# Layer 0's values and layer 1's x into token form: 32x32 block transposes on VectorE and a pass through DRAM in place of transposes on TensorE

## The chip, the core and the metric

One core of a Trainium2 chip runs the kernel: TensorE (PE, its weight loads listed as PEld), VectorE (DVE), ScalarE (ACT), GpSimd (POOL) and SyncE (SP), which issues nearly all DMA. The metric is device time of one execution in microseconds. The kernel before was timed three times: 1389.19, 1389.40 and 1389.46 us, median 1389.4.

## The reference: what is computed

Two residual layers work on 272 tokens (16 learned meta tokens and 256 frames) of width 2048, in float32. Pad slots that the reference puts in front are masked there and are not stored by the kernel.

Layer 0 projects the tokens once and splits the result. Four heads of gated linear attention (GLA) have keys of 256 and values of 512; eight stick-breaking heads (SB) have width 128. In both, a matrix of scores between tokens multiplies the values `v`:

```python
o_intra = jnp.einsum('bchts,bcshv->bcthv', scores, v)
outs.append(jnp.einsum('bhqk,bhkd->bhqd', w, v[:, :, :k_len].astype(jnp.float32)))
```

Layer 1 is a Mamba-2 mixer (SSD) with 8 groups of 8 heads of 64. Its `x` is convolved over time, passed through SiLU, and multiplied by a step `dt` for each token and head; then a matrix of decays and scores multiplies it:

```python
xdt = x * dt[..., None]
y_diag = jnp.einsum('bctsgh,bcsghp->bctghp', l_mat * cb[..., None], xdt)
```

Each layer ends with an output projection, a residual and a layer norm.

In all three places the sum runs over source tokens `s`, so the values must lie with tokens on partitions ("token form"). The projections deliver them with channels on partitions. Something must transpose them.

## The kernel before

**Units and projections.** The weights come in units of 128x2048 floats (1 MB), in a list written out in the program. SP loads them ahead of use into three buffers `raw` (L144). ACT rounds each half of a unit to `whi` (L159); DVE, and for some late units POOL, takes the rest `wlo` (L160). There are five buffers of halves. A unit of an input projection gives 128 channels for all tokens: 16 slices of the contraction, three matmuls each (L178, L179, L180, the products hi·hi, hi·lo, lo·hi), 48 matmuls that add up in one PSUM bank `pj` with channels on partitions and 272 (or 256) tokens on columns. Output units of layer 1 are 24 matmuls of 512 columns (L494 to L496).

**What sets the order.** When a unit is done, its post function takes the PSUM bank over. What follows (attention, gates, the SSD scan) is written as generators, which are stepped once a quarter of a unit; a `yield` is thus a delay in the program's order. A scheduler then sets the final order of instructions on each engine, and each engine runs its own list strictly in order. An instruction that waits holds up whatever stands behind it on the same engine. This is also true of SP: a load that waits for a free buffer, or for another transfer to land, holds up the loads behind it.

**Values of layer 0.** `post_gv` (GLA, four units a head, worked off in pairs) and `post_sv` (SB, one unit a head) copy the bank to `vraw` on ACT (L623, L761). `to_tokens` transposes it on PE with the identity as the moving operand: two 128x128 blocks (L587) and the last 16 tokens (L588) for each unit, into a bank `po`. ACT rounds the result to `gvh` (L596, L592), DVE takes the rest `gvl` (L597 to L599). `values` (L608 and after) multiplies them with the score matrix.

**x of layer 1.** Four units of a group fill `xt`. The convolution and SiLU are done in pairs (DVE L1050, L1057, L1061). After the second pair `x_path` waits five more steps, transposes on PE (L1173, eight blocks; L1177, four of 16 tokens), and DVE multiplies each result straight out of PSUM by `dt` from `est` and `est2` into `xd` (L1186, four) and `xd2` (L1192, four). The SSD mix multiplies `M` by `xd` on PE (L1235). `M` is made on DVE and ACT (L1105, L1106, L1108) from `ebc`, a copy of the group's decays on all partitions, which SP loads from the DRAM tile `edr` (L1072) into the one buffer with the tag `hacc` (272 x 16 floats a partition; `ebc` fills 8 x 416 of these 4352).

In all there are 168 transposes on PE: 48 at L587, 24 at L588, 64 at L1173 and 32 at L1177.

## Time and profile before

| | |
|---|---|
| median of three runs | 1389.4 us |
| the profiled execution's own time | 1389.59 us |
| its span, first to last instruction | 1387.7 us |
| PE busy | 1379.2 us, 99% |
| DVE busy | 1017.3 us, 73% |
| ACT busy | 771.7 us, 56% |
| POOL busy | 260.6 us, 19% |
| granted TensorE clock | 1.000 |
| DMA over the span | 249.83 MB, mean 180 GB/s |

Layer 0 fills about the first half of the span; the first SSD transposes stand shortly after 763 us. Records of PE overlap: matmuls are pipelined, and a matmul's record is longer than the distance to the next one. What an instruction adds to PE's list is therefore read from the distance between starts. In a row of a timeline stand the start, the duration, engine, line, operation, output and inputs, shapes and count, and in brackets the idle time ahead of it and what ended it. In a row of groups stand the count, then the busy sum and the mean in ns, then idle time ahead. A DMA row gives the count, KB each and the median us from issue to landing.

### The profile page before, as it was taken

The numbers are of one execution on the slowest core, as the hardware profiler recorded it, in microseconds if no ns is written. First come the engines' busy times: TensorE is split into PE (matmuls) and PEld (weight loads), VectorE is DVE, ScalarE is ACT, GpSimd is POOL, SyncE is SP. The second block draws the span as 40 slices with busy tenths as digits, with TensorE's granted clock in tenths as the row PEclk, the third lists the DMA queues.
The fourth block names the chain that finished last, engine by engine and source line by source line (L and its number), as shares of the span: only waits on it lengthen the run. The fifth ranks groups of instructions, "written<-read, shape, count | busy, mean of one in ns | idle before, by whom it ended". The sixth has DMA issues, their size and how long they took to land.

```text
span 1387.7 us, 26097 instructions
## 1 busy us (share of the span) xinstructions
PE 1379.2 (99%) x10715; PEld 1328.3 (96%) x10715; DVE 1017.3 (73%) x1690; ACT 771.7 (56%) x1149; POOL 260.6 (19%) x253
## 2 busy tenths in 40 slices
PE   9999999999999999999999999999999999999998
PEld 8999999999999999999999999899898999989986
DVE  7857575574565565557899999787877778867687
ACT  6645454454345544556587677565565655656551
POOL 0000010100101000113500153331322323133221
PEclk9999999999999999999999999999999999999999
DMA  8544544445454445544354655465555556455561
GB/s 320 185 161 156 181 154 171 163 156 179 156 179 156 153 152 179 174 151 148 122 199 169 251 202 201 158 256 174 213 180 187 197 187 228 164 200 185 179 216 61
DMA packets 38007, 249.83 MB, mean 180 GB/s; under 512 B 4288, under 2 KB 6144, under 8 KB 9472
## 3 DMA queue, kind: packets, MB, share of 16 engines
q1 hardware_dynamic: 37168, 247.38, 51.0%
q8 instruction: 84, 1.38, 0.4%
q10 hardware_dynamic: 720, 0.79, 0.2%
q14 instruction: 35, 0.29, 0.1%
HBM read 245.94 MB, written 2.20 MB: 179 GB/s over the span
## 4 chain that ended last, share of the span: by engine, by line
PE 94%; DVE 3%; DMA 1%; ACT 1%; POOL 1%; issue 0%; SPq 0%; ACTq 0%; POOLq 0%; DVEq 0%
PE pj L179 25%; PE pj L178 25%; PE pj L180 25%; PE pj L494 4%; PE pj L496 4%; PE pj L495 4%; PE po L1235 1%; PE po L608 1%; DVE wlo L160 1%; PE po L1173 0%; DMA raw<-in_wts 0%; PE po L587 0%; PE z L1123 0%; POOL yu L1246 0%; DVE M L1105 0%
## 5 line engine op out<-in xcount | busy, mean ns | idle before, releaser
L178 PE MATMUL pj<-xhi,whi 128*128 128x272 f32 (+4 forms) x2560 | 732.1, 286 | 1.3 <-DVE fix L936 0.5
L179 PE MATMUL pj<-xlo,whi 128*128 128x272 f32 (+4 forms) x2560 | 730.8, 286 | 0.0
L180 PE MATMUL pj<-xhi,wlo 128*128 128x272 f32 (+4 forms) x2560 | 730.1, 286 | 0.0
L159 ACT ACTIVATE whi<-raw 128x1024 fp32r<-128x1024 f32 (+2 forms) x434 | 449.6, 1039 | 423.8 <-PE pj L179 350.7
L160 DVE TENSOR_TENSOR wlo<-raw,whi 128x1024 fp32r<-128x1024 f32 (+2 forms) x405 | 503.3, 1247 | 242.0 <-ACT whi L159 237.4
L178 PEld LDWEIGHTS pj<-xhi,whi 128*128 128x128 f32 x2560 | 482.1, 189 | 3.7 <-ACT whi L159 0.9
L179 PEld LDWEIGHTS pj<-xlo,whi 128*128 128x128 f32 x2560 | 482.1, 188 | 1.5 <-DVE wlo L160 0.4
L180 PEld LDWEIGHTS pj<-xhi,wlo 128*128 128x128 f32 x2560 | 481.9, 188 | 1.0 <-issue 0.8
L178 PE MATMUL pj<-mixh,whi 128*128 128x272 f32 x384 | 110.5, 289 | 0.0
L180 PE MATMUL pj<-mixh,wlo 128*128 128x272 f32 x384 | 110.5, 288 | 0.0
L179 PE MATMUL pj<-mixl,whi 128*128 128x272 f32 x384 | 110.4, 288 | 0.0
L160 POOL TENSOR_TENSOR wlo<-raw,whi 128x1024 fp32r<-128x1024 f32 x29 | 73.0, 2517 | 192.6 <-ACT whi L159 192.6
L494 PE MATMUL pj<-whi,yh 128*128 128x512 f32 (+1 forms) x240 | 93.3, 389 | 0.0
L495 PE MATMUL pj<-wlo,yh 128*128 128x512 f32 (+1 forms) x240 | 92.6, 386 | 0.0
L496 PE MATMUL pj<-whi,yl 128*128 128x512 f32 (+1 forms) x240 | 92.2, 386 | 0.0
L261 POOL TENSOR_TENSOR gr<-gr,gsc 128x1088 f32<-128x1088 f32 x6 | 15.4, 2568 | 308.2 <-ACT gsc L260 308.2
L179 PEld LDWEIGHTS pj<-mixl,whi 128*128 128x128 f32 x384 | 72.3, 188 | 0.2
L180 PEld LDWEIGHTS pj<-mixh,wlo 128*128 128x128 f32 x384 | 72.3, 188 | 0.1
L178 PEld LDWEIGHTS pj<-mixh,whi 128*128 128x128 f32 x384 | 72.2, 188 | 0.1
L503 DVE SCALAR_TENSOR_TENSOR acc<-pj,rr,acc 128x512 f32<-128x512 f32 (+1 forms) x65 | 46.5, 734 | 13.9 <-PE pj L496 13.9
L496 PEld LDWEIGHTS pj<-whi,yl 128*128 128x128 f32 x240 | 45.1, 188 | 9.1
L494 PEld LDWEIGHTS pj<-whi,yh 128*128 128x128 f32 x240 | 45.1, 188 | 9.0
(351 smaller groups left out, 1472.2 us busy)
## 6 DMA issues: line engine op xcount, KB each, us to landing
raw<-in_wts SPq DMA_DIRECT2D x212, 1024.0 KB, 4.8
ebc<-edr SPq DMA_DIRECT2D x8, 1664.0 KB, 6.7
raw<-in_wts SPq DMA_DIRECT2D x9, 256.0 KB, 6.4
hacc<-in_xT SPq DMA_DIRECT2D x7, 272.0 KB, 5.3
early<-in_wts SPq DMA_DIRECT2D x2, 512.0 KB, 6.5
lg<-in_lnr SPq DMA_DIRECT2D x1, 1024.0 KB, 4.7
lb<-in_lnr SPq DMA_DIRECT2D x1, 1024.0 KB, 5.3
out_h<-acc SPq DMA_DIRECT2D x2, 384.0 KB, 2.4
```

Of the source, the lines that this page charges most:

```text
L159: self.nc.scalar.activation(hi, src, AF.Copy)
L160: eng.tensor_tensor(lo, src, hi.bitcast(F32), op=ALU.subtract)
L178: mm(ps, whi, xhi, start=first, stop=False)
L179: mm(ps, whi, xlo, start=False, stop=False)
L180: mm(ps, wlo, xhi, start=False, stop=last)
L261: mul(c, c, e, op=ALU.mult)
L494: mm(ps, yh[:, kk, tt], hi[:, k, :], start=kk == 0, stop=False)
L495: mm(ps, yh[:, kk, tt], lo[:, k, :], start=False, stop=False)
L496: mm(ps, yl[:, kk, tt], hi[:, k, :], start=False, stop=kk == 3)
L503: self.nc.vector.scalar_tensor_tensor(a, ps, r[:, t : t + 1], a, op0=ALU.mult, op1=ALU.add)
L608: mm = lambda r, a, b, start=False, stop=False: self.nc.tensor.matmul(o[:, r], a, b, start=start, stop=stop, skip_group_check=True)
L1235: pin(mm(ov[p][i * 64 : (i + 1) * 64, jj, t0:S], xd[:, s, h * 64 : (h + 1) * 64], M[:, h, c0:c1], start=(s, jj) == (0, 0), stop=False, **gk,))
```

## The change

A transpose of 128x128 is made of two steps: transposing each 32x32 block in place on DVE, and then moving blocks between partitions, which DMA does by a pass through DRAM.

**Layer 0.** `v_blocks` transposes the blocks straight out of the projection's PSUM bank into `vt` (L586, 256 elements a partition; L587, the 32 columns that hold the last 16 tokens). There is one buffer `vt`, and no `vraw`. `to_tokens` then has SP write `vt` to a DRAM tile (L600, L601) and read it back in five parts: four for the 32-partition strips of the two big token tiles (L604; runs of 128 bytes for an SB head, 256 for a GLA pair), one for the last 16 tokens (L606). The reads come back into `vt` itself. ACT and DVE then split as before, from SBUF (L612 to L617).

**Layer 1.** `x_path` transposes after each of the two pairs (L1186, 512 elements a partition; L1187, 64). The result `xs` lies in the unused tail of the group's `ebc` buffer. After the second pair SP writes 512 KB and 64 KB (L1194, L1195), reads four parts back into `xs` (L1198, runs of 512 bytes) and two into `xd2` (L1202). DVE multiplies by `dt` from SBUF (L1214, four; L1221, two, in place). The five steps of delay are gone, and the wait for the step sizes is now a wait until the group's `ebc` has been asked for. `load_decay` of the next group, which takes the same buffer, comes behind the reads of this group. `est2` is held twice, at partitions 0 and 32, and `cpk` shrinks from 384 to 360 columns.

```diff
+    def v_blocks(self, ps, i, n):
+        if i == 0:
+            self.vt = self.lp.tile([P, 768], F32, tag="vt", name=self.nm("vt"))
+        o = self.vt[:, : 256 * n].rearrange("q (b c x) -> q b c x", c=n, x=32)[:, :, i, :]
+        self.nc.vector.transpose(o, ps[:, :256].rearrange("p (b x) -> p b x", x=32))
+        self.nc.vector.transpose(self.vt[:, 512 + 32 * i : 544 + 32 * i], ps[:, 240:T])
+        return self.vt
...
     def to_tokens(...):
-            for t in range(2):
-                nc.tensor.transpose(pts[i][:, t * P : (t + 1) * P], raw[:, t * P : (t + 1) * P], self.ident)
-            nc.tensor.transpose(pts[0][:16, 256 + i * P : 256 + (i + 1) * P], raw[:, 256:272], self.ident)
-        nc.scalar.activation(v2[:16, w], t2, AF.Copy)
-            nc.scalar.activation(vh[:, :, c], p, AF.Copy)
-            nc.vector.tensor_tensor(vl[:, :, c], p, vh[:, :, c].bitcast(F32), op=ALU.subtract)
...
+        sync.dma_start(d.rearrange("p t b x -> (p t) (b x)"), blk)
+        sync.dma_start(d9.rearrange("p t x -> (p t) x"), s9)
+        v = blk.rearrange("q (s p x) -> q s p x", s=2, p=4)
+        for b in range(4):
+            sync.dma_start(v[32 * b : 32 * b + 32], d[:, :, b::4].rearrange("p t s x -> t s p x"))
+        t2 = vt[:16, 512 : 512 + P * n].rearrange("q (p x) -> q p x", p=4)
+        sync.dma_start(t2, d9[:, 16:].rearrange("p t x -> t p x"))
+        yield
+        yield
...
+        act(chan(v2[:16, w]), cols(t2), AF.Copy)
+        for t in range(2):
+            act(chan(vh[:, t, w]), cols(v[:, t]), AF.Copy)
+            vec.tensor_tensor(chan(vl[:, t, w]), cols(v[:, t]), chan(vh[:, t, w].bitcast(F32)), op=ALU.subtract)
...
     def load_decay(self, g):
-        eb = self.hp.tile([P, HPG, 416], F32, tag="hacc", name=self.nm("ebc"))
+        eb = self.hp.tile([P, KT * T], F32, tag="hacc", name=self.nm("ebc"))
+        self.cur["xs", g] = eb[:, HPG * 416 :].rearrange("p (b c x) -> p b c x", c=4, x=32)
...
     def x_path(self, g, j):
-        if g == 0:
-            yield from _wait(self.tasks["dt"])
+        while ("ebc", g) not in self.cur:
+            yield
+        vec.transpose(xs[:, :, j : j + 2, :].rearrange("p b c x -> p c b x"), xt[:, j : j + 2, :S].rearrange("p c (b x) -> p c b x", x=32))
+        vec.transpose(x9[:, j : j + 2, :], xt[:, j : j + 2, 240:T])
+        yield
         if j == 0:
             return
-        for _ in range(5):
-            yield
...
+        nc.sync.dma_start(d.rearrange("p t b x -> (p t) (b x)"), xs.rearrange("q b c x -> q (b c x)"))
+        nc.sync.dma_start(d9.rearrange("p t c x -> (p t) (c x)"), x9.rearrange("q c x -> q (c x)"))
+        for b in range(4):
+            nc.sync.dma_start(
+                xb[32 * b : 32 * b + 32], d[:, :, b::4].rearrange("p t s x -> t s p x")
+            )
+        for i in range(2):
+            nc.sync.dma_start(
+                self.xd2[32 * i : 32 * i + 16].rearrange("t (n a) (b x) -> t n (a b) x", n=2, b=2),
+                d9[:, 16:, i::2].rearrange("p t n x -> t n p x"),
+            )
...
+                vec.tensor_tensor(o, x, e.broadcast_to([P, 4, 2, 32]), op=ALU.mult)
...
+            vec.tensor_tensor(x, x, e.broadcast_to([16, 2, 2, 64]), op=ALU.mult)
```

**Where instructions stand now.** SP gains seven DMA for each GLA pair and each SB head, and eight for each SSD group; its list goes from 256 rows to 352, rows of one kind side by side counted once. On SP at SB head 1 (`raw` are weight loads, `vt` the block-transposed values, `vdr` the DRAM tile) the changed program has:

```order
L144 DMA raw_5407<-in_wts 128x2048
L144 DMA raw_5504<-in_wts 128x2048
L144 DMA raw_5580<-in_wts 128x2048
L600 DMA vdr_5450<-vt_5404 128x256
L601 DMA vdr_659_5451<-vt_5404 128x32
L604 DMA vt_5404<-vdr_5450 32x8x32 x4
L606 DMA vt_5404<-vdr_659_5451 16x4x32
L144 DMA raw_5665<-in_wts 128x2048
```

Before, only the weight loads stood there. The writes now stand behind one weight load and the reads ahead of the next.

ACT at the same head, before:

```order
L761 ACTIVATE vraw_5378<-pj_5298 128x272
L572 ACTIVATE s0h_5372<-sbe_5336 128x432
L159 ACTIVATE whi_5513<-raw_5380 128x1024
L592 ACTIVATE v_148<-po_5423 16x128
L596 ACTIVATE gvh_5294<-po_5423 128x2x128
L803 ACTIVATE spad<-z_64 128x432
L159 ACTIVATE whi_5549<-raw_5470 128x1024
L745 ACTIVATE qe_5467<-pj_5382 128x272
```

and changed:

```order
L572 ACTIVATE s0h_5398<-sbe_5362 128x432
L159 ACTIVATE whi_5543<-raw_5407 128x1024
L818 ACTIVATE spad<-z_64 128x432
L159 ACTIVATE whi_5583<-raw_5504 128x1024
L761 ACTIVATE qe_5501<-pj_5409 128x272
L614 ACTIVATE gvh_5320<-vt_5404 128x128 x2
L612 ACTIVATE v_148<-vt_5404 16x128
L572 ACTIVATE s0h_5475<-spad 128x432
```

The copy to `vraw` is gone, and the split to `gvh` has moved behind the next unit's weight half and the next head's `qe`. On PE, 90 to 92 projection matmuls now stand between the end of an SB head's `sv` unit and its first matmul of values for heads 1, 2, 3, 5, 6 and 7 (80 to 104 before), and 104 for heads 0 and 4 as before.

DVE at SSD group 3, before:

```order
L1061 TENSOR_TENSOR xt_11029<-xt_11029,xcl_11279 128x544
L160 TENSOR_TENSOR wlo_11441<-raw_11327,whi_11440 128x1024
L160 TENSOR_TENSOR wlo_11479<-raw_11387,whi_11478 128x1024
L1057 TENSOR_SCALAR xcl_11420<-gz_11325 128x512
L1186 TENSOR_TENSOR xd_11030<-po_11406,est 128x256 x2
L1186 TENSOR_TENSOR xd_11030<-po_11407,est 128x256 x2
L1192 TENSOR_TENSOR xd_8126<-z_64,est_8718 16x128 x4
L160 TENSOR_TENSOR wlo_11507<-raw_11387,whi_11506 128x1024
```

and changed (`ebc_10958` here is its tail `xs`):

```order
L1077 TENSOR_TENSOR xt_11107<-xt_11107,xcl_11360 128x544
L1186 STREAM_TRANSPOSE ebc_10958<-xt_11107 128x2x8x32
L1187 STREAM_TRANSPOSE x_1359_11265<-xt_11107 128x64
L160 TENSOR_TENSOR wlo_11556<-raw_11484,whi_11555 128x1024
L1073 TENSOR_SCALAR xcl_11505<-gz_11408 128x512
L160 TENSOR_TENSOR wlo_11584<-raw_11484,whi_11583 128x1024
L160 TENSOR_TENSOR wlo_11617<-raw_11552,whi_11616 128x1024
L1214 TENSOR_TENSOR xd_11108<-ebc_10958,est 128x4x64 x4
L1221 TENSOR_TENSOR xd_8208<-xd_8208,est_8798 16x256 x2
```

The block transposes stand right behind the last SiLU product, and the products with `dt` have moved two weight halves further back. The writes and reads stand between the two on SP, the reads behind one more weight load:

```order
L1194 DMA xdr_11429<-ebc_10958 128x1024
L1195 DMA xdr_1379_11430<-x_1359_11265 128x128
L144 DMA raw_11659<-in_wts 128x2048
L1198 DMA ebc_10958<-xdr_11429 32x8x128 x4
L1202 DMA xd_8208<-xdr_1379_11430 16x8x32 x2
L144 DMA raw_11741<-in_wts 128x2048
L1090 DMA ebc_11901<-edr 128x3328
```

Before, the next group's decay load (L1072) stood behind this group's last read of `ebc` by DVE; now also behind the reads of x.

88 lines of the change are left out of this document (39 added, 49 removed).

## The prediction, on record before the changed kernel ran

> **What bounds the kernel now.** I read the page's busy row first, then the row of slices, then what PE waited for, then the busy time by stretches.
>
> ```profile
> PE 1379.2 (99%) x10715; PEld 1328.3 (96%) x10715; DVE 1017.3 (73%) x1690; ACT 771.7 (56%) x1149; POOL 260.6 (19%) x253
> DVE  7857575574565565557899999787877778867687
> PE po L1393 <- ACT diag L1328: 1.2, 1, 1.2
> ```
>
> PE is busy for 1379.2 of the span's 1387.7 us, and its longest wait is 1.2 us. So the kernel lasts as long as PE's list of instructions, and an instruction taken off PE is worth its own length, as long as nothing else is the limit where it stood. The slices say where that is in doubt: DVE stands at 9 in slices 22 to 25, some 730 to 870 us. Cut into windows (window, length, then busy time and instructions of PE, weight loads, DVE, ACT and POOL, then clock, DMA share, GB/s):
>
> ```profile
> 730.00:760.00 30.00, 29.17 (x245) 28.42 (x243) 28.78 (x55) 21.51 (x35) 3.01 (x3) 1.00 0.49 170
> 760.00:790.00 30.00, 30.00 (x237) 27.69 (x238) 29.20 (x59) 21.60 (x30) 4.72 (x3) 1.00 0.63 232
> 790.00:830.00 40.00, 39.80 (x358) 37.84 (x355) 39.67 (x81) 27.21 (x46) 18.53 (x12) 1.00 0.59 207
> 890.00:975.00 85.00, 85.00 (x645) 80.02 (x643) 67.02 (x104) 50.17 (x70) 23.65 (x18) 1.00 0.54 194
> ```
>
> From 730 to 830 DVE is busy for 97.65 of 100 us (28.78 + 29.20 + 39.67), with PE modelled as busy too. PE runs 237 matmuls in the 30 us of the second window, where even the 0.123 us of its wider matmuls (next part) would make 244: it runs at DVE's pace there. From 890 on DVE has 18 of 85 us free and PE has none. So there are two regimes: a saturated stretch that holds SSD groups 0 and 1, and a PE-bound rest.
>
> **What leaves PE.** The timeline of PE around the transposes of SSD group 3, of stick-breaking (SB) head 1 and of the first GLA pair gives the price, not by the records' lengths, which overlap, but by the distance of starts:
>
> ```profile
> 955.69 0.28 PE L178 MATMUL pj<-xhi,whi 128*128 128x256 f32 x1
> ...
> 956.26 0.28 PE L180 MATMUL pj<-xhi,wlo 128*128 128x256 f32 x1
> 956.38 1.04 PE L1173 MATMUL po<-ident,xt 128*128 128x128 f32 x8
> 957.25 0.60 PE L1177 MATMUL z<-ident,xt 128*16 128x128 f32 x4
> ...
> 957.81 0.28 PE L179 MATMUL pj<-xlo,whi 128*128 128x256 f32 x1
> ```
>
> ```profile
> 461.22 0.28 PE L178 MATMUL pj<-xhi,whi 128*128 128x272 f32 x1
> ...
> 461.71 0.29 PE L179 MATMUL pj<-xlo,whi 128*128 128x272 f32 x1
> 461.84 0.38 PE L587 MATMUL po<-ident,vraw 128*128 128x128 f32 x2
> 462.05 0.27 PE L588 MATMUL po<-ident,vraw 128*16 128x128 f32 x1
> ...
> 462.29 0.29 PE L178 MATMUL pj<-xhi,whi 128*128 128x272 f32 x1
> ```
>
> ```profile
> 46.99 0.29 PE L180 MATMUL pj<-xhi,wlo 128*128 128x272 f32 x1
> 47.11 0.38 PE L587 MATMUL po<-ident,vraw 128*128 128x128 f32 x2
> ...
> 47.68 0.29 PE L179 MATMUL pj<-xlo,whi 128*128 128x272 f32 x1
> ```
>
> Undisturbed, a 256-column matmul comes every 0.114 us (0.57 over five) and a 272-column one every 0.123 us (0.49 over four). SSD: 956.26 to 957.81 is 1.55 us with two matmuls' own steps in it, so 1.55 - 0.23 = 1.32 us a group, times 8 = 10.6. SB: 0.58 - 0.25 = 0.33 a head, times 8 = 2.6. GLA: 0.69 - 0.25 = 0.44 for four transposes; the pair's other two L587 stand elsewhere, and I take 0.30 for them, just under SB's 0.33 for three; 0.74 times 8 pairs = 5.9. Together **19.1 us** off PE (bounds 15 and 20: without, and with, all of the restart behind each little group). ACT also loses 24 copies to vraw.
>
> **What DVE gains.** The trace of before has no block transpose. The nearest rows are
>
> ```profile
> L1186 DVE TENSOR_TENSOR xd<-po,est 128x256 f32<-128x256 f32 x32 | 11.7, 414 | 0.9 <-PE po L1173 0.9
> L1192 DVE TENSOR_TENSOR xd<-z,est 16x128 f32<-16x128 f32 x32 | 7.6, 272 | 0.1
> L1061 DVE TENSOR_TENSOR xt<-xt,xcl 128x544 f32<-128x544 f32 x16 | 13.0, 814 | 12.2 <-ACT xcl L1060 12.0
> L1057 DVE TENSOR_SCALAR xcl<-gz 128x512 f32<-128x512 f32 x16 | 6.7, 419 | 0.0
> L1011 DVE RECIPROCAL dt_scr<-dt_scr 64x272 f32<-64x272 f32 x1 | 1.8, 1837 | 0.0
> ```
>
> For 512 elements the low bound is L1057's 0.42 us, the high bound the reciprocal's 1837/272 = 6.75 ns an element, 3.5 us. I take 0.65, between L1057 and L1061 (0.81 for 544), because a transpose reads one tensor and streams it. A group then loses 4 x 0.41 + 4 x 0.27 = 2.7 by the means, or 2.4 as the overlapping run of eight below stands in the timeline, and gains two transposes of 0.65 and two small ones of 0.2 (1.7), four products of 256 elements from SBUF at 0.38 (L1061's rate; 1.5) and two 16x256 ones of 0.35 (0.7): 3.9, net **+1.5 us a group**; by the bounds +1.0 and +7.6. Outside the saturated stretch that is covered: six groups' 9 us lie in DVE's free fifth, and layer 0's +0.55 a head and +1.1 a pair in slices that read 5 to 8.
>
> The Trainium skill, "VectorE: DVE Perf Modes", section "The three transpose paths", gives 390 ns on TensorE and 311 ns on VectorE for 128x128. By it four blocks' worth of 512 columns would take an estimated 1.24 us, the two saturated groups would pay 2.4 us more, and the sum would be about 1381. This trace shows TensorE's side otherwise: eight L1173 in 1.04 us.
>
> **The saturated stretch.** Groups 0 and 1 have their transposes in it, so PE's 2 x 1.32 = 2.6 us are not gained there, and DVE's 2 x 1.5 = 3.0 us lengthen it.
>
> **The round trip through DRAM.** SP issues writes, waits for them to land, issues reads; the reader waits again. Prices:
>
> ```profile
> raw<-in_wts SPq DMA_DIRECT2D x212, 1024.0 KB, 4.8
> ebc<-edr SPq DMA_DIRECT2D x8, 1664.0 KB, 6.7
> out_h<-acc SPq DMA_DIRECT2D x2, 384.0 KB, 2.4
> edr<-dt_scr SPq DMA_DIRECT2D x1, 104.0 KB, 2.1
> q1 hardware_dynamic: 37168, 247.38, 51.0%
> q10 hardware_dynamic: 720, 0.79, 0.2%
> ```
>
> A write of 128 to 512 KB is 2.1 to 2.4 us by edr and out_h. A set of four reads is 1024 short runs, 64 on each of 16 engines. q10 moved 720 packets in 0.2% of 16 x 1387.7 us, 62 ns a packet of 1.1 KB, so 64 of them are at most 4.0 us; by bytes (q1: 247.38 MB in 51% of 16 engines, 22 GB/s each) SB's 128 KB are 0.4 us. I take 2.5 to landing.
>
> SB head 1, on the clock of before:
>
> ```profile
> 458.93 0.38 ACT L761 ACTIVATE vraw<-pj 128x272 f32<-128x272 f32 x1
> 466.29 0.38 ACT L745 ACTIVATE qe<-pj 128x272 fp32r<-128x272 f32 x1
> 471.06 0.28 PE L608 MATMUL po<-s0l,gvh 128*128 128x272 f32 x1
> 456.69 0.33 SPq L144 DMA_DIRECT2D raw<-in_wts  x1
> ```
>
> The weight load ahead of the write in SP's order was issued at 456.69, so SP is free. The projection ends by 458.9, transposes by 459.3, the write is issued (0.33) and lands by 461.9, five reads at 0.33 to 0.46 each go out until 464 and land by 466.9. ACT, in the new order, comes to gvh behind qe, at 466.7; gvh is done at 467.7. PE wants it 90 to 92 matmuls after the projection, or 11.2 us, near 470: a margin of about 2.5 us. The next weight load waits behind the reads for 1 us, against three buffers of lead. Cost 0.
>
> SSD group 3:
>
> ```profile
> 957.67 1.41 DVE L1186 TENSOR_TENSOR xd<-po,est 128x256 f32<-128x256 f32 x4
> 961.50 0.33 SPq L144 DMA_DIRECT2D raw<-in_wts  x1
> 968.40 1.23 DVE L160 TENSOR_TENSOR wlo<-raw,whi 128x1024 fp32r<-128x1024 f32 x1 [4.16 <-ACT whi L159]
> 974.13 2.93 PE L1235 MATMUL po<-M,xd 128*64 128x256 f32 x32
> 977.11 0.35 DVE L1105 TENSOR_SCALAR M<-ebc,est 128x256 f32<-128x256 f32 x1 [1.49 <-PE po L1235]
> ```
>
> The transposes end near 957.8, where the products began. The write lands by 961. The reads stand behind the 1 MB load of 961.50 in SP's order, so they share the engines with its 4.8 us and land between 966.8 and 969.4. DVE comes to the products near 964.3 and stands 2.5 to 5 us; behind it queue weight halves (wlo), for which PE waits only after the halves already split are used up, and DVE had 4.16 us idle ahead of 968.40. Products take 2.5 us, until 969.3 to 971.9; L1235 needs them at 974.13: 2 to 5 us of margin. The next group's decay load must now wait for these reads, since they land in the tail of the same buffer; issued after 969 it lands by 975.6 to 980 (6.7 us and the queue), and M asks at 977.11: up to 3 us of DVE, covered by the 18 free. In the saturated stretch there is no cover; there I put 1.5 us for group 1's wait, half of the steady group's bound of 3, and 1 us in all for weight loads that SP issues later behind its waits.
>
> **Sum.** The profiled execution took 1389.6 us (span 1387.7 and 1.9 around it); the runs' median is 1389.4. 1389.6 - 19.1 + 2.6 + 3.0 + 1.5 + 1.0 = 1378.6; I say **1378.5 us**.
>
> **Rivals.** (1) *The round trip of the SB heads outlasts its 11 us.* Mechanism: four reads of 128-byte runs, with SP waiting in between. For it: no row of before prices so short a run, and 2.5 us is thin. Against it: 64 runs an engine at q10's 62 ns stay at 4.0 us, 1.5 later than taken. Each us past the margin stops PE once in 8 heads, so the gain of 11 us is gone when a head's reads land 2.5 + 1.4 = 3.9 us later than I took; at 6 us it is 3.5 x 8 = 28: about 1406. The Trainium skill speaks for it: "DMA: Bandwidth & Descriptors", "Specifications", wants 512 B at least for the full rate, and the page above calls a plain strided copy 19 times slower than the crossbar's 1309 ns, which would be an estimated 25 us a 128x128 block, far past the margin. No run here shows that yet; the runs of 32 elements are not single ones. (2) *The saturated stretch pays nothing*: transposes at L1057's rate and earlier splits hide it, and the whole gain stays, 1389.6 - 19.1 = 1370.5, to 1373 with one group's stall. For it: PE is shown as 30.00 of 30 busy in it. Against: 97.65 of 100 on DVE. (3) *Block transposes at the reciprocal's rate*: two groups pay 2 x 6.1 = 12 us more, 1378.5 + 12 = 1390.5, no change. Against: one operation that is known to be slow is a far row.
>
> **How the numbers follow.** My forecast 0.46, its own range 1373 to 1385; (2) 0.25; (1) 0.17, most of it slower, since it does not stop at the break-even; (3) 0.12, split over the three signs. About 0.2%, 2.8 us, is what a measurement can tell from no change: under 1386.6 faster, over 1392.2 slower. Faster 0.46 + 0.25 + 0.01 = 0.72; same 0.02 of (1) and 0.08 of (3) = 0.10; slower 0.15 + 0.03 = 0.18. Eight times in ten: 1371, which leaves out only the end of (2), to 1394, which takes in (3) and the start of (1).
>
> **What would show it.** Right: no transposes on PE and its count down by 168; waits of PE still under 2 us; L608 as far from its projection as its matmuls take; L1186 near 0.65 us; reads landing in 2 to 4 us; DVE over 97% from 730 to 830 and that stretch longer by 4 to 6 us. Wrong: waits of PE on gvh in eight heads (1), the stretch no longer than before (2), L1186 over 2 us (3), or PE waiting for wlo or M at each group, which I priced at nothing.

## The result, and the profile after

The changed kernel took 1405.1 us (median of four runs, 1402.0 to 1406.1) against 1389.4 for the kernel before: a ratio of 1.0111 (95% interval 1.0097 to 1.0124), 15.8 us slower. I had forecast 1378.5 and, eight times in ten, 1371 to 1394.

The profiled execution took 1405.95 us, its span 1404.1, at a mean granted clock of 0.996. The page's busy row:

```profile
PE 1385.0 (99%) x10547; PEld 1334.1 (95%) x10547; DVE 1040.1 (74%) x1763; ACT 767.2 (55%) x1133; POOL 260.3 (19%) x253
```

PE has 168 instructions fewer, as the change says, and yet is busy for 5.8 us longer (1379.2 before). So two things must be told apart: PE waits more (the span grew by 16.4, PE's busy time by 5.8), and the instructions left on PE take longer. What PE and DVE waited for (in total, times, longest):

```profile
DVE xd L1214 <- DMA ebc<-xdr: 31.8, 7, 7.8
...
PE pj L494 <- DVE acc L503: 6.5, 4, 2.5
PE z L1141 <- ACT bcp L1112: 2.1, 1, 2.1
```

Before, PE's longest wait was 1.2 us. Now output units of layer 1 (L494) wait four times for their PSUM bank, which DVE (`acc`, L503) empties late, and DVE itself stands 31.8 us, 4.5 on average in each of seven groups, for `x` to come back from DRAM. The windows (length; busy time and instructions of PE, weight loads, DVE, ACT, POOL; clock, DMA share, GB/s):

```profile
56.00:456.00 400.00, 400.00 (x3193) 398.54 (x3192) 257.51 (x437) 192.43 (x269) 32.26 (x35) 1.00 0.53 178
...
830.00:870.00 40.00, 37.00 (x292) 35.30 (x292) 33.81 (x60) 23.75 (x37) 14.98 (x12) 0.96 0.61 214
...
865.00:870.00 5.00, 4.08 (x22) 4.08 (x23) 4.94 (x6) 4.23 (x8) 2.68 (x2) 0.68 0.56 188
870.00:875.00 5.00, 5.00 (x33) 5.00 (x33) 4.96 (x11) 3.97 (x9) 1.32 (x3) 0.64 0.54 170
```

From 830 to 870 PE ran 292 matmuls, where it ran 338 before in the same stretch of the clock; right behind the wait of 2.1 us on `bcp`, which the trace has at 865.9, the granted clock was near 0.66 for ten microseconds. The first row will matter most: in 400 us of layer 0 without a gap, PE got through 3193 matmuls. Before:

```profile
56.00:456.00 400.00, 400.00 (x3244) 398.19 (x3241) 250.94 (x408) 195.67 (x281) 32.20 (x35) 1.00 0.49 166
```

The 3244 included transposes, 48 at GLA's pairs, so equal counts would mean a loss already. Here the count even fell, with PE never idle. PE's timeline gives the price of one matmul. Before, 16 starts apart:

```profile
64.00 0.28 PE L178 MATMUL pj<-xhi,whi 128*128 128x272 f32 x1
...
65.98 0.28 PE L179 MATMUL pj<-xlo,whi 128*128 128x272 f32 x1
```

and after, the same sixteen:

```profile
63.98 0.29 PE L178 MATMUL pj<-xhi,whi 128*128 128x272 f32 x1
...
65.99 0.28 PE L179 MATMUL pj<-xlo,whi 128*128 128x272 f32 x1
```

1.98 us against 2.01. Over all undisturbed pairs of neighbours the mean step of the 272-column projection matmuls was 123.4 ns before and 125.7 after, and of the 256-column ones 114.2 and 117.3. The matmuls on `mixh` and `yh`, with operands from other tiles, kept theirs (123 to 124, and 226 to 227). The 320 matmuls of 260 columns went the other way, 120.0 to 118.5. Some 5450 matmuls by 2.3 ns and 1500 by 3.1 make 17 us, more than the whole loss, and the 260-column ones give 0.5 back.

The groups of the new work, as far as I had priced them (count, busy sum, mean ns, idle ahead), and the DMA (count, KB each, median us from issue to landing):

```profile
L1214 DVE TENSOR_TENSOR xd<-ebc,est 128x256 f32<-128x256 f32 x32 | 15.8, 551 | 31.8 <-DMA ebc<-xdr 31.8
L1186 DVE STREAM_TRANSPOSE ebc<-xt 128x512 f32<-128x512 f32 x16 | 11.3, 705 | 0.1
```

```profile
xdr<-ebc SPq DMA_DIRECT2D x8, 512.0 KB, 5.6
ebc<-xdr SPq DMA_DIRECT2D x32, 128.0 KB, 5.0
...
vt<-vdr SPq DMA_DIRECT2D x32, 32.0 KB, 2.2
```

DVE's prices are near my estimates (0.705 for 0.65, and 0.201 for 0.2 at L1187). The write and the reads of `x` are not: 5.6 and 5.0 us, where I had 2.1 to 2.4 and 2.5.

In what follows I often compare two traces matmul by matmul: the projections (L178 to L180) and the output units (L494 to L496) are one list in all these programs, so the start of the nth of them in one trace less its start in the other gives how far the one has fallen behind at that place. I call this the lag.

### The profile page after: what moved, and what is told of

Same layout as the page of the kernel before. It is cut to its first block, busy times and chain, and to the rows that moved or that the text cites. A ratio compares the mean times of both kernels' runs of the same rounds, so it can differ in the third digit from the quotient of the medians.

```text
span 1404.1 us, 26095 instructions
## 1 busy us (share of the span) xinstructions
PE 1385.0 (99%) x10547; PEld 1334.1 (95%) x10547; DVE 1040.1 (74%) x1763; ACT 767.2 (55%) x1133; POOL 260.3 (19%) x253
## 4 chain that ended last, share of the span: by engine, by line
PE 81%; DMA 7%; DVE 7%; issue 2%; ACT 1%; SPq 1%; POOL 0%; ACTq 0%; DVEq 0%; POOLq 0%
PE pj L179 23%; PE pj L178 23%; PE pj L180 23%; DMA xdr<-ebc 3%; PE pj L494 2%; PE pj L496 2%; PE pj L495 2%; DMA ebc<-xdr 2%; DMA ebc<-edr 2%; PE po L626 1%; DVE M L1123 1%; DVE wlo L160 1%; DVE M L1124 1%; SPq L1198 1%; ACT whi L159 1%
## 5 line engine op out<-in xcount | busy, mean ns | idle before, releaser
L178 PE MATMUL pj<-xhi,whi 128*128 128x272 f32 (+4 forms) x2560 | 736.2, 288 | 2.2 <-ACT gz L1228 1.2
L180 PE MATMUL pj<-xhi,wlo 128*128 128x272 f32 (+4 forms) x2560 | 734.3, 287 | 0.0
L178 PEld LDWEIGHTS pj<-xhi,whi 128*128 128x128 f32 x2560 | 483.0, 189 | 4.5 <-ACT gz L1228 1.4
L180 PEld LDWEIGHTS pj<-xhi,wlo 128*128 128x128 f32 x2560 | 482.8, 189 | 0.2
L178 PE MATMUL pj<-mixh,whi 128*128 128x272 f32 x384 | 110.8, 290 | 0.0
L180 PE MATMUL pj<-mixh,wlo 128*128 128x272 f32 x384 | 110.5, 288 | 0.0
L494 PE MATMUL pj<-whi,yh 128*128 128x512 f32 (+1 forms) x240 | 94.4, 393 | 6.5 <-DVE acc L503 6.5
L496 PE MATMUL pj<-whi,yl 128*128 128x512 f32 (+1 forms) x240 | 92.9, 388 | 0.0
L180 PEld LDWEIGHTS pj<-mixh,wlo 128*128 128x128 f32 x384 | 72.3, 188 | 0.0
L178 PEld LDWEIGHTS pj<-mixh,whi 128*128 128x128 f32 x384 | 72.2, 188 | 0.2
L494 PEld LDWEIGHTS pj<-whi,yh 128*128 128x128 f32 x240 | 45.5, 189 | 17.1 <-ACT M L1126 8.1
L496 PEld LDWEIGHTS pj<-whi,yl 128*128 128x128 f32 x240 | 45.4, 189 | 9.3
L495 PEld LDWEIGHTS pj<-wlo,yh 128*128 128x128 f32 x240 | 45.5, 190 | 8.8
```

The costliest lines, as they stand in the source:

```text
L178: mm(ps, whi, xhi, start=first, stop=False)
L180: mm(ps, wlo, xhi, start=False, stop=last)
L494: mm(ps, yh[:, kk, tt], hi[:, k, :], start=kk == 0, stop=False)
L495: mm(ps, yh[:, kk, tt], lo[:, k, :], start=False, stop=False)
L496: mm(ps, yl[:, kk, tt], hi[:, k, :], start=False, stop=kk == 3)
```

## The experiments

### Is it the size of one small tile? e1_cpk_only

`cpk` holds small constants. The change cut it from 384 to 360 columns, 96 bytes a partition. All that is allocated behind it (`raw`, `whi`, `wlo`, `hacc`, the pools of the layers) moves down by 96 bytes; `xhi` and `xlo` are allocated ahead of it and stay. My theory was that this move slows the matmuls; the rival, that the new DMA or DVE traffic does. The experiment is the kernel before with this alone, and its instructions stand in the same order on every engine.

```diff
-        self.cpk = C([P, 384], "cpk")
+        self.cpk = C([P, C_END], "cpk")
```

> The kernel before with one edit: cpk is 360 columns wide, not 384. Every buffer behind it, the weight halves among them, moves 96 bytes down; xhi and xlo, the operands that stream through PE, stay. No instruction is added, removed or moved. Theory A (address): in the changed kernel's trace the 272-column matmuls of L178 to L180 come every 125.7 ns, before every 123.3 ns, from the first units on, and the ones that stream mixh or yh, which moved together with the weights, are as before; the distance between streamed operand and weights sets the step. Then this kernel is slow too: 5450 matmuls x 2.4 ns + 1500 x 3.3 ns = 18 us, 1405 to 1409, with 125.7 ns a step. Theory B (the step is slower because of the added transfers or of a clock that is granted less, 0.996): 1389.4, 123.3 ns.

Measured: 1405.96 us (1404.97 to 1406.78), ratio 1.0113 (1.0095 to 1.0130). The same 400 us of layer 0:

```profile
56.00:456.00 400.00, 400.00 (x3198) 398.16 (x3197) 247.30 (x400) 192.98 (x277) 32.27 (x35) 1.00 0.48 164
```

46 matmuls fewer than before, with no transposes moved and no new DMA; 46 by 0.123 is 5.7 us in these 400. An edit of one number, which changes no instruction, costs 16.5 us, as much as the whole change. The steps with the 0.5 given back make about as much.

### Can it be undone from the other side? e2_after_realigned

In the change, `xhi` and `xlo` are read from a later or earlier column of their rows (there is slack of 48 columns, 192 bytes). Moving the start down by 24 columns, 96 bytes, restores the distance between the operand that streams and the weights, though neither address is what it was.

```diff
-X0, X1, XM = 48, 32, 48
+X0, X1, XM = 24, 8, 48
```

> The changed kernel with one edit: xhi and xlo are used from 24 and 8 columns into their tiles, not 48 and 32, so that they too move 96 bytes down and stand to the weights as before. The order of instructions is the same on every engine. Theory A: the step is back at 123.3 ns and about 18 us are back: 1405 - 18 = 1387, with what is left, 1387 - 1370 = 17 us over the pure gain, in the stretch 810 to 1010 where layer 1 waits for its round trips. Theory B: 1405, step 125.7 ns.

Measured: 1392.6 us (1387.6 to 1397.6), ratio 1.0022 (1.0007 to 1.0038), so 12.6 less than the changed kernel. The window and PE's longest wait:

```profile
56.00:456.00 400.00, 400.00 (x3241) 398.54 (x3240) 261.11 (x442) 196.21 (x275) 33.83 (x38) 1.00 0.54 181
```

```profile
PE pj L494 <- DVE acc L503: 7.3, 4, 3.9
```

The step is back at 123.4 ns, now with the transposes gone. What is left of the loss is in the waits, and these vary from run to run more than the kernel before does.

### Which distances are slow? e8_shift_32_64, e9_shift_192_128, e10_shift_160_32

Before and e2 have a distance from the start of the streamed operand to the start of the weights of 64, modulo 256 bytes, in both layers; the change and e1 have 224. Three variants of the kernel before with other starts give two distances each, one for a layer. They were measured once each, and their steps count here, not their times.

```diff
-X0, X1, XM = 48, 32, 48
+X0, X1, XM = 40, 16, 48
```

```diff
-X0, X1, XM = 48, 32, 48
+X0, X1, XM = 0, 0, 48
```

```diff
-X0, X1, XM = 48, 32, 48
+X0, X1, XM = 24, 40, 48
```

> The kernel before with the streamed operands moved alone: layer 0 uses xhi and xlo from column 40 (32 bytes lower), layer 1 from column 16 (64 bytes lower); the same instructions in the same order. If it is a distance that is no multiple of 64 bytes that slows PE (96 is none): layer 0 goes at 125.7 ns a 272-column matmul, layer 1 at 123.3; 1389.4 + 8 to 9 = 1398. If any other distance than that of before is slow: both, 1406. If only the 96 bytes were: 1389.4.

> The kernel before, streamed operands moved alone: layer 0 uses columns from 0 (192 bytes lower than before), layer 1 from 0 (128 bytes lower). The run with 32 and 64 bytes lower showed 123.5 ns for 32 and 126.6 ns for 64, and the change's own 96 in the other direction 125.7 (by the distance from operand to weights, taken modulo 256: 64 before, 96, 128 and 224). If the step goes by that distance and is fast only around 64 to 96: distances 0 and 192 are both slow, 125 to 127 ns. If it is fast in every second 64 bytes: 0 is slow, 192 fast.

> The same with layer 0 from column 24 (96 bytes lower, distance 160 modulo 256) and layer 1 from column 40 (32 bytes higher, distance 32). The change moved the weights by 96 bytes towards the operand; this moves the operand by 96 away. If only the size of the step counted, layer 0 would be slow by 2.4 ns as in the change. If the distance counts, 160 lies behind 128 and should be slow, 32 is the edge of the fast side and is open: 123.3 or 125.7.

Measured: 1402.3, 1406.4 and 1409.8 us. The mean step of the 272-column projection matmuls, by the distance modulo 256 that the addresses give:

| distance | where | mean step, ns |
|---|---|---|
| 64 | before, e2, e3: both layers | 123.4 |
| 96 | e8, layer 0 | 123.5 |
| 0 | e9, layer 0 | 125.6 |
| 32 | e10, layer 1 | 125.6 |
| 160 | e10, layer 0 | 126.3 |
| 224 | after, e1: both layers | 125.7 |
| 128 | e8, layer 1 | 126.6 |
| 192 | e9, layer 1 | 126.6 |

The distances are worked out from the addresses; the numbers in the labels are not these throughout. I had thought that a multiple of 64 or of 32 would turn out to be the rule; neither holds, since 0, 128 and 192 are slow, and 96 is fast. Two neighbours of eight are fast. That the distance between the two operands decides, not the address of the weights or of the operand alone, rests on e1 (weights moved, slow), e8 to e10 (operand moved, slow in five of six places) and e2 (both moved, fast): e1 and e2 have the same address of the weights, e10 and e2 the same start of the operand in layer 0 (column 24), and of these only e2 is fast. The table is for 272 columns. The 260-column matmuls stand at other distances, since their operand starts 12 columns later: 80 before and 240 after, and there 240 is the faster one. Why, no trace shows: a matmul record is the same 0.28 to 0.29 us either way. The Trainium skill, "SBUF — State Buffer", section "A bandwidth-pool intuition that's wrong (but worth ruling out)", gives the weight load a "2nd independent read port"; by it the two reads need not meet, so one would not expect where they start to matter. These rows show that it does; whether the two reads meet, no run here shows.

### Layer 0 alone: e3_layer0_only

The change's layer 0 with its short `cpk` and the restored distance, and layer 1 as before.

```diff
-X0, X1, XM = 48, 32, 48
+X0, X1, XM = 24, 8, 48
...
     def x_path(self, g, j):
-        vec.transpose(xs[:, :, j : j + 2, :].rearrange("p b c x -> p c b x"), xt[:, j : j + 2, :S].rearrange("p c (b x) -> p c b x", x=32))
+        if g == 0:
+            yield from _wait(self.tasks["dt"])
...
+                    pin(nc.tensor.transpose(
+                        pt[:, t * 256 + i * P : t * 256 + (i + 1) * P], xt[:, jj + i, t * P : (t + 1) * P], self.ident
+                    ))
```

> Layer 0's part alone (block transposes and round trip for the values of GLA and SB, x of layer 1 by PE as before), with cpk at 360 and the 24/8 columns of the run before. Removes 72 of the 168 transposes, 8.5 us by the prediction's count. If layer 0's round trips are hidden: 1389.4 - 8.5 = 1381. If the rival of the prediction is at work (reads of short runs outlast the gap in eight SB heads), 1389 or more, with waits of PE before the values' matmuls.

Measured: 1383.4 us (1382.9 to 1387.2), ratio 0.9958 (0.9942 to 0.9973): 6.0 faster. By the lag, GLA's eight pairs give 5.4 us (from -0.4 ahead of the first to -5.8 behind the last; I had 5.9), and an SB head 0.38 (I had 0.33). But the eight heads together give only 0.7, because in two stretches, 515 to 555 and 650 to 680 us, PE's step is longer with nothing moved. Fourteen steps there in e3:

```profile
529.75 0.29 PE L178 MATMUL pj<-xhi,whi 128*128 128x272 f32 x1
...
531.52 0.29 PE L180 MATMUL pj<-xhi,wlo 128*128 128x272 f32 x1
```

and in the kernel before:

```profile
529.83 0.29 PE L179 MATMUL pj<-xlo,whi 128*128 128x272 f32 x1
...
531.55 0.29 PE L178 MATMUL pj<-xhi,whi 128*128 128x272 f32 x1
```

1.77 us against 1.72, that is 126 ns a step against 123, at the same addresses as in the rest of e3. It sets in after an interruption of the row of projection matmuls and ends with another. These stretches cost some 2.2 us, and the first of them is in e2, e7 and e13 to e15 too. What puts PE into this slower step I can't tell. The profiled execution is the slowest of the five (1387.2): in it PE stands 2.1 us for `ysq` until 806.3, the granted clock is 0.68 from 805 to 810, and the lag goes from -6.5 to -3.0.

The round trip of layer 0 itself is hidden. SB head 1 in the changed kernel, on its own clock:

```profile
458.89 0.33 SPq L600 DMA_DIRECT2D vdr<-vt  x1
462.27 2.54 SPq L604 DMA_DIRECT2D vt<-vdr  x4
466.72 0.51 ACT L614 ACTIVATE gvh<-vt 128x128 fp32r<-128x128 f32 x2
470.60 0.29 PE L626 MATMUL po<-s0h,gvh 128*128 128x272 f32 x1
```

The write goes out at 458.89, the reads from 462.27 to 464.8, `gvh` is done at 467.2, and PE takes it at 470.60; PE has no wait on `gvh` anywhere.

### Layer 1 alone: e4_layer1_only

The change's layer 1, with layer 0 and the 384 columns of `cpk` as before.

```diff
-        self.cpk = C([P, C_END], "cpk")
+        self.cpk = C([P, 384], "cpk")
...
-    def to_tokens(self, vt, n, vh, vl, v2, j):
+    def to_tokens(self, raws, vh, vl, v2, j):
...
+                nc.tensor.transpose(pts[i][:, t * P : (t + 1) * P], raw[:, t * P : (t + 1) * P], self.ident)
+            nc.tensor.transpose(pts[0][:16, 256 + i * P : 256 + (i + 1) * P], raw[:, 256:272], self.ident)
```

> Layer 1's part alone (values of layer 0 by PE as before), cpk at 384 columns as before, so that no operand moves against the weights. Removes 96 transposes, 10.6 us. If the round trip of x is hidden as predicted: 1379 + 5. If the stalls of groups 1 to 3 seen in the changed kernel (DVE stands 31.8 us in front of its products, 7 times) reach PE: 1389.4 - 10.6 + 17 = 1396.

Measured: 1395.3 us (1392.2 to 1401.1), ratio 1.0044 (1.0029 to 1.0060): 5.9 slower, where the terms of the prediction for layer 1 (10.6 - 2.6 - 3.0 - 1.5 - 1.0) gave 2.5 faster. The three parts, -6.0 (e3), +5.9 (e4) and +16.5 (e1), add up to 16.4 against 15.8 for the whole. So this is where the second error lies. SP's list at group 2 in e4:

```profile
884.20 0.33 SPq L1179 DMA_DIRECT2D xdr<-ebc  x1
...
886.87 2.53 SPq L1183 DMA_DIRECT2D ebc<-xdr  x4
...
895.45 0.33 SPq L1075 DMA_DIRECT2D ebc<-edr  x1
```

DVE at the same place, and then what PE waited for in the whole run:

```profile
893.48 1.95 DVE L1199 TENSOR_TENSOR xd<-ebc,est 128x256 f32<-128x256 f32 x4 [2.77 <-DMA ebc<-xdr]
...
901.99 2.39 DVE L1108 TENSOR_SCALAR M<-ebc,est 128x256 f32<-128x256 f32 x1 [1.30 <-DMA ebc<-edr]
...
908.54 1.39 DVE L503 SCALAR_TENSOR_TENSOR acc<-pj,rr,acc 128x512 f32<-128x512 f32 x2
```

```profile
PE pj L494 <- DVE acc L503: 5.8, 3, 2.9
...
PE po L1246 <- DVE xd L1199: 3.3, 2, 1.8
...
DVE xd L1199 <- DMA ebc<-xdr: 29.7, 7, 6.4
```

Read as a chain: SP needs 2.53 us only to issue four reads, 0.63 each. The last has landed at 893.48, 9.3 us after the write was issued. DVE, which had stood for 2.77 us, makes `xd` until 895.43. Only then may SP issue the next group's decays, at 895.45, since they go into the same buffer. They are there at 901.99, and `M` begins. In the kernel before:

```profile
892.17 0.35 DVE L1105 TENSOR_SCALAR M<-ebc,est 128x256 f32<-128x256 f32 x1 [1.49 <-PE po L1235]
...
900.27 1.40 DVE L503 SCALAR_TENSOR_TENSOR acc<-pj,rr,acc 128x512 f32<-128x512 f32 x2
```

`M` begins 9.8 us earlier there, and the output units' `acc` behind it (L503) is reached at 900.27; in e4 only at 908.54, though PE itself was then about 3 us late (the first L494 of this row of output units starts at 885.5, and at 882.3 before). PE waits for both: for `xd` twice, and for the banks that `acc` empties three times, once for 2.28 us at 909.42, with the granted clock at 0.66 from 910 to 915. The same happens again at group 4: `acc` stands behind `M` there too and is reached at 1081.24, PE waits 2.93 us for it until 1082.13, the clock is 0.66 from 1080 to 1090, and the lag goes from 6.7 to 12.8 there, the largest single loss of this run.

### Is the decay load's wait the cause? e5_decay_unchained

One persistent tile takes the place of a new one for each group, so that the next decays no longer wait until the tail `xs`, which they don't touch, has been read.

```diff
-        eb = self.hp.tile([P, KT * T], F32, tag="hacc", name=self.nm("ebc"))
+        if "eb" not in self.cur:
+            self.cur["eb"] = self.hp.tile([P, KT * T], F32, tag="hacc", name="ebc")
+        eb = self.cur["eb"]
```

> Layer 1's part alone, as in the run before, with one edit: the decay buffer and its tail are one tile for the whole layer, not a new one for each group, so that the next group's decay load waits only for this group's readers of the decays, not for the reads of x that land in the tail. Theory A: in the run before, the chain reads of x, products, decay load, M is what stops PE (M of the group after begins at 901.99, 9.8 us later than in the kernel before, and the output units then wait 2.4 to 3.1 us for an accumulation queued behind it on DVE, and the clock falls after it). Then those waits are gone, what is left is PE's wait for xd in groups 1 and 2 (3.3 us in all): 1395.3 - 11 = 1384. Theory B: the wait for x itself (29.7 us of DVE in front of its products) delays the weight halves, and the decay load is hidden: 1395, no change.

Measured: 1395.7 us (1390.7 to 1400.1), ratio 1.0042 (1.0028 to 1.0057), no different from e4. The waits:

```profile
PE pj L178 <- ACT gz L1215: 6.1, 1, 6.1
PE pj L494 <- DVE acc L503: 2.2, 3, 1.2
...
DVE xd L1201 <- DMA ebc<-xdr: 33.7, 7, 7.7
```

By its time the theory falls; by its trace it was half right. Behind 850 us the wait on `acc` went from 5.8 to 2.2, and the lag, which grew from 2.4 to 9.2 us in e4, here went from 5.1 to 3.7. But a single wait of 6.1 us had appeared at 814 us, with a granted clock of 0.84 and 0.50 in the two windows of 5 us from 815 on. There are thus two places of loss in layer 1, and this one is ahead of the other.

### Are the four reads the cause? e6_one_read

The short runs go into the write (four writes of 512-byte runs), and one read of 2 KB runs takes the place of four.

```diff
-        nc.sync.dma_start(d.rearrange("p t b x -> (p t) (b x)"), xs.rearrange("q b c x -> q (b c x)"))
-        for b in range(4):
+        for p in range(4):
             nc.sync.dma_start(
-                xb[32 * b : 32 * b + 32], d[:, :, b::4].rearrange("p t s x -> t s p x")
+                d[:, :, :, p, :].rearrange("s b t x -> t (s b) x"),
+                xs[32 * p : 32 * p + 32].rearrange("t b c x -> t b (c x)"),
             )
+        nc.sync.dma_start(
+            xb.rearrange("q s p x -> q s (p x)"), d.rearrange("s b t p x -> (b t) s (p x)")
+        )
```

> As the run before, and the pass through DRAM turned round: four writes of 512-byte runs, one for each 32 partitions, lay the blocks out in the order in which they are read, and one read of 2 KB runs takes the place of the four. SP then issues one read (0.6 us) behind its wait, not four (2.5 us), so x should land some 2 us earlier: DVE's 29.7 us in front of the products fall by 7 x 2 = 14, PE's 3.3 us of waiting for xd go, and the time is 1384 - 3 = 1381. If not the issue but the place behind a 1 MB weight load on the same 16 engines sets the landing, DVE's wait stays near 30 us and the time stays that of the run before.

Measured: 1385.4 us (1382.0 to 1388.3), ratio 0.9974 (0.9964 to 0.9983).

```profile
DVE xd L1204 <- DMA ebc<-xdr: 17.9, 7, 5.0
...
PE pj L178 <- ACT gz L1218: 1.9, 1, 1.9
```

DVE's wait for `x` is nearly halved, 33.7 to 17.9, and 10.3 us are won against e5. Not all of it is the reads' own price: the wait at 814 us shrank from 6.1 to 1.9, and this time the clock stayed at 1.00 behind it.

### The whole change, mended: e7_all_mended

Distance restored, decays unchained, one read; the rest as in the change.

> The whole change, with the operands realigned (24/8 columns), the decay load unchained and the one read: 1389.4 - 6 (layer 0 alone, measured) - 8 (layer 1 alone, if the run before comes to 1381) = 1375. If the repairs of layer 1 do nothing: 1392, as the realigned run.

Measured: 1379.1 us (1378.7 to 1382.3), ratio 0.9936 (0.9923 to 0.9948). It is close to my forecast for the unmended change, which is a coincidence: it has three mends that the forecast knew nothing of, and the wait on `gz` is still there, 2.0 us that end at 811.0 on its own clock.

### How much would a free round trip be worth? e12_no_trip

e4 without the write and the reads: DVE multiplies what its block transposes left, so the blocks are never moved between partitions and `x` stands in the wrong places. The work on PE, DVE and ACT is the same.

```diff
-        nc.sync.dma_start(d.rearrange("p t b x -> (p t) (b x)"), xs.rearrange("q b c x -> q (b c x)"))
-        nc.sync.dma_start(d9.rearrange("p t c x -> (p t) (c x)"), x9.rearrange("q c x -> q (c x)"))
-        for b in range(4):
...
-        for i in range(2):
```

> Layer 1's part alone (as the run that measured 1395), with the pass through DRAM left out: no write and no read, the products take the transposed blocks where they lie (so x stands in the wrong place; the work on DVE, ACT and PE is the same). Theory A (the trip's latency, and what queues behind the wait for it, is the whole loss): 1389.4 - 10.6 + 1 to 3 for DVE's extra 1.5 us in the two saturated groups = 1380. Theory B (DVE's extra work in the saturated stretch is the loss): still 1390 or more.

Measured: 1389.9 us (1388.4 to 1390.9), ratio 0.9994 (0.9985 to 1.0003): no change against before, even with the trip gone.

```profile
PE pj L178 <- ACT gz L1200: 9.2, 1, 9.2
```

By the lag, groups 2 to 7 give what PE's transposes cost. All of it, and no more, is lost in one place: from 809 to 830 us the lag goes from -1.7 to +8.0, with this one wait and a clock of 0.81, 0.50 and 0.67 in the three windows of 5 us from 815 on; from there it falls to -0.3 by the end. So the place near 815 us is no matter of the round trip.

### Which group makes the wait near 815? e13_mixed, e14_from_group3, e15_from_group2, e16_group0_only

First e7 with groups 1 and 2 back on PE, as these are the ones being prepared there:

```diff
     def x_path(self, g, j):
+        if g in (1, 2):
+            if j:
+                yield from self.x_by_pe(g, j, xt, xd)
+            return
```

(`x_by_pe` holds the old transposes and products, five steps of delay included.)

> The mended whole change (1379.1) with groups 1 and 2 alone transposed on PE as before, the other six through DRAM. Aligned matmul by matmul, the mended run gained 1.96 us at group 0, 1.33 at each of groups 3 to 7, and lost 2.3 and 2.6 at groups 1 and 2, where DVE is full and x is waited for. If that loss belongs to the trip in the full stretch: 1379.1 - 5 = 1374. If the stretch is slow for another reason there (the order that the scheduler finds): 1379 or more.

Measured: 1380.8 us (1379.6 to 1381.1), ratio 0.9926 (0.9912 to 0.9940). It misses what I expected: the wait on `gz` did not go, it grew to 4.5 us.

```profile
PE pj L178 <- ACT gz L1273: 4.5, 1, 4.5
```

With groups 1 and 2 cleared, group 0 was left. Two kernels put group 0 on PE too (the first three groups, and the first two), and a third takes group 0 alone through DRAM, with layer 0 and `cpk` as before:

```diff
-        if g in (1, 2):
+        if g < 3:
+            if g == 0:
+                yield from _wait(self.tasks["dt"])
```

```diff
-        if g in (1, 2):
+        if g < 2:
+            if g == 0:
+                yield from _wait(self.tasks["dt"])
```

```diff
-        if g in (1, 2):
+        if g:
```

> The mended whole change with groups 0, 1 and 2 on PE as before and groups 3 to 7 through DRAM. If group 0's move (its transposes and products on a full DVE, and the order of DVE's list that follows) brings the wait of 4.5 to 9.2 us near 815: it is gone, layer 1 keeps 5 x 1.33 = 6.7 us and layer 0 its 6: 1389.4 - 12.7 = 1376.7. If the stretch stalls with any change to the lists behind it: 1380, as the run with groups 1 and 2 on PE.

> The same with group 2 through DRAM too. Without the trip group 2 gained 1.5 us, in the unmended layer 1 it cost 9.2. If the mended trip is short enough: 1376.7 - 1.4 = 1375.3; if PE still waits for its x: 1378 or more.

> Layer 1's part for group 0 alone, mended, all else as before. If group 0's move brings the wait near 815: 1389.4 - 1.3 + 2 to 9 = 1390 to 1397, with PE waiting there for ACT's gz. If not: 1388.

Measured: e14 1376.0 us (1374.7 to 1376.7), ratio 0.9904 (0.9887 to 0.9921); e15 1375.0 us (1373.4 to 1375.4), ratio 0.9897 (0.9883 to 0.9912); e16 1395.0 us (1394.5 to 1395.6), ratio 1.0044 (1.0029 to 1.0059). Beside the runs of before of the same series (median 1388.9), one group out of eight, moved, costs 6.1 us; the other seven do not need to move for it. How, the rows of e16 show, first DVE, then ACT, then two windows:

```profile
789.95 1.08 DVE L1208 TENSOR_TENSOR xd<-ebc,est 128x256 f32<-128x256 f32 x3
...
810.61 1.88 DVE L1138 TENSOR_TENSOR M<-M,cb 128x800 f32<-128x800 f32 x2
...
814.46 0.46 DVE L1301 SCALAR_TENSOR_TENSOR yu<-xt,cpk,po 128x256 f32<-128x256 f32 x1
```

```profile
819.11 1.21 ACT L1258 ACTIVATE gz<-pj 128x256 f32<-128x256 f32 x4 [0.69 <-POOL yu L1302]
```

```profile
815.00:820.00 5.00, 0.48 (x3) 0.46 (x3) 4.96 (x9) 4.14 (x9) 3.09 (x3) 0.72 0.39 129
820.00:825.00 5.00, 5.00 (x27) 5.00 (x27) 4.20 (x7) 1.28 (x5) 2.95 (x1) 0.59 0.80 272
```

and the same three instructions in the kernel before:

```profile
772.08 0.96 DVE L1192 TENSOR_TENSOR xd<-z,est 16x128 f32<-16x128 f32 x4
...
804.01 0.47 DVE L1245 SCALAR_TENSOR_TENSOR yu<-xt,cpk,po 128x256 f32<-128x256 f32 x1
```

```profile
807.48 0.36 ACT L1202 ACTIVATE gz<-pj 128x256 f32<-128x256 f32 x1
```

Before, the last products for group 0 were made by 773.0 us; through DRAM the first three only by 791.0, in the one stretch where DVE has no free time. The mix on PE that takes them ends only 2 us later, though (its last eight matmuls begin at 794.9, before at 793.0). The outputs `yu` on DVE fall back much further: the last stands at 814.46 instead of 804.01, now behind group 1's `M` (L1138), of which the same products began only at 808.59 before. POOL's product with `yu` frees the one buffer `gz`, and ACT can copy the next projection bank into it only at 819.11 instead of 807.48. So PE stands in front of that bank from about 815: the window from 815 to 820 has three matmuls in it. 4.5 us of wait are put down to `gz` (L1258), and in the next five microseconds the clock is at 0.59, and PE gets through 27 matmuls where 44 of 114 ns would fit.

So it is the place on DVE's list that counts, more than how late the products are. In e12, without a trip, DVE makes them only 4 us later than before, and the wait is the longest of all:

```profile
774.46 2.52 DVE L1186 TENSOR_TENSOR xd<-ebc,est 128x256 f32<-128x256 f32 x4
...
815.15 0.99 DVE L1136 TENSOR_TENSOR M<-M,cb 128x800 f32<-128x800 f32 x1
...
820.49 0.47 DVE L1243 SCALAR_TENSOR_TENSOR yu<-xt,cpk,po 128x256 f32<-128x256 f32 x1
```

In all nine kernels that move group 0 (the change, e2, e4 to e7, e12, e13, e16) two of its four `yu` stand behind the first of these products of group 1, and PE waits 1.2 to 9.2 us on `gz`; in the other eight all four stand ahead of it, and PE has no such wait. Why the scheduler's order falls this way, and why the wait is 2 us in one kernel and 9 in another, stays open.

In e15, the fastest of all, this wait is gone, and PE's longest wait is 1.1 us:

```profile
PE 1363.9 (99%) x10571; PEld 1313.8 (96%) x10571; DVE 1040.9 (76%) x1759; ACT 766.4 (56%) x1133; POOL 262.1 (19%) x253
```

Its span is 1373.7 us. That version, layer 0 and groups 2 to 7 through DRAM with the distance restored, decays unchained and one read, beats the kernel before by 13.9 us (same series) and the change by 30.

## Why the prediction was wrong, point by point

**The step that failed first is one I didn't take: what the smaller `cpk` does.** I took 0.123 and 0.114 us a step from the trace of before, and used them for what leaves PE; that the 7000 matmuls that stay would keep these steps was assumed and not said. They went to 0.1257 and 0.1173, and this alone is +16.5 us (e1), more than the 11.0 us that all my terms together gave. The rows of before could not have priced it, as every projection matmul of 272 or 256 columns there has the same distance to its weights; `X0`, `X1` and the shift of 48 columns at L167 set it. But the line was in the diff, and a range that rests on two steps by thousands of matmuls should have had a term for what changes them.

**What leaves PE: right.** GLA 5.4 us against 5.9; SB 0.38 a head against 0.33; SSD, for groups 3 to 7 by the lag, 1.3 to 1.7 each against 1.32. PE's list lost about what I said it would. Of what the SB heads gave, the stretches of the slower step took back about 2.2.

**The transposes' price: right.** 0.705 us for 0.65, 0.201 for 0.2. The products of 256 elements took 0.551 by the mean (0.418 by the median, the longest 2.6), where I had 0.38, which is 0.7 us a group more, in time that DVE had free outside the stretch. Rival 3 falls.

**Layer 0's round trip at cost 0: right, and rival 1 falls.** My chain for SB head 1 had the reads out until 464, `gvh` done at 467.7 and PE near 470; the rows have 464.8, 467.2 and 470.60. Reads of 32 KB in 128-byte runs landed in 2.2 us, and those of 64 KB in 256-byte runs in 2.4. The 512 B of the Trainium skill's "DMA: Bandwidth & Descriptors", "Specifications", and the 19 times of its "VectorE: DVE Perf Modes", "The three transpose paths", did not decide here: two or three microseconds for a short read are what 11 us of lead hide.

**SSD's round trip, "covered by the 18 free": wrong.** The terms were mis-sized: the write 5.6 us by its median for 2.1 to 2.4, the reads 5.0 for 2.5 (6.1 in e4), 0.63 us a read on SP for 0.33 to 0.46. The rows I took them from were one transfer (`edr`) and two at the very end (`out_h`); whether it is the loads beside them that make the difference, no run separates. DVE's stall was 4.5 us a group on average; five of the seven lay within the 2.5 to 5 that I gave, the other two were 6.9 and 7.8. What failed is where I stopped asking: I asked whether `xd` and `M` would be in time, and compared DVE's free time with its stall as sums. I did not follow the instructions that queue behind: the stall makes the next decays late, these make `M` late, and the `acc` of the output units stands behind `M` (e4: 5.8 us of waits on `acc`, 3.3 on `xd`). e5 and e6 bear this out for the stretch behind 850 us: unchained, the wait on `acc` fell to 2.2, and with one read DVE's stand fell to 17.9.

**The saturated stretch: right that it pays, wrong in what.** I had DVE's 97.65% and put 3.0 us of DVE work, 1.5 us for group 1 and 1.0 for SP on it. DVE is at 97% there in the changed kernel too (28.98, 28.20 and 39.88 us in the three windows from 730 to 830). But the price is no sum of DVE work. It is the order of DVE's list: with group 0 moved, its last outputs stand behind group 1's `M`, and a single buffer stays taken until they are done: 6.1 us (e16), and up to 9.2 us of PE's wait (e12). I had put nothing on that path. I had charged the wait to group 1, the one with the steady group's bound; e13 repeats the same error and e16 settles it. Rival 2, that the stretch pays nothing, falls too.

**What would make it wrong.** I had named "PE waiting for wlo or M at each group". It waited for `acc`, `xd` and `gz`, in a few groups. So the place was watched, but for the wrong instructions.

## What to carry to other kernels

When a diff changes the size of any tile on the chip, ask what is allocated behind it and compare the step of the same matmuls in both traces, before any other theory; in this kernel the start of the weights relative to the streamed operand is worth 2% of each matmul. Price a detour through DRAM by transfers that run beside the same loads, and follow it on each in-order engine to the first instruction behind the stalled one that PE needs, not to the result alone. Where an engine has no free time, look at what the list puts ahead of the results that free a buffer, and not only at the work that is added; here 1.7 us of added work on DVE for group 0 (4.1 us of rows in e16, 2.45 before) became 6.1 us of loss, and six groups of eight were worth more than all eight.

## What the runs showed of the hardware

- **The step of a matmul depends on the distance of its two operands in memory.** Modulo 256 bytes, 64 and 96 gave 123.4 and 123.5 ns for 272 columns; 0, 32, 128, 160, 192 and 224 gave 125.6 to 126.6. I know of no reason, and only these eight were tried. For 260 columns, 80 gave 120.0 and 240 gave 118.5.
- **A short stop of PE can cost a second time, through the clock.** From the stall near 815 us on, the granted clock in e16 was 0.72 and 0.59 in two windows of 5 us, in the changed kernel 0.68 and 0.64 behind the 2.1 us on `bcp`, in e4 0.66 behind the 2.28 us on `acc`. But behind the stalls of 1.9 and 2.0 us in e6 and e7 it stayed at 1.00. Of the twelve waits of PE between 1.7 and 3.0 us in these traces, seven have such a dip right behind them and five have none. This may be why the runs of e4 and e5 lie 9 us apart, and those of e14, without such a stall, 2. The Trainium skill, "TensorE: Matmul & The Clock Gate", section "What's actually happening", puts the half rate behind an idle window of about 3.4 us that runs freely. That the dips come and go with the same stall fits a free-running window; that stalls of 2 us bring them does not fit its length.
- **PE can stay in a slower step, 126 to 127 ns for 123, at unchanged addresses** for 30 to 40 us after an interruption (e3). What starts and ends it is open.
- **SP took 0.63 us to issue a read of short runs**, twice the 0.33 of a plain load, and four of them are 2.5 us in which no weight load goes out.
